# Between two decoder layers: block sums on VectorE, a fifth leading pair, ascending pool groups and two more buffers

## The chip, the cores and the metric

The kernel runs on one core of a Trainium2 chip. The metric is the device time of one execution in microseconds, the median of several. TensorE (PE) multiplies; VectorE (DVE), ScalarE (ACT) and GpSimd (POOL) do the elementwise work; almost all transfers are issued from SyncE's queue (SP).

## The reference

Two decoder layers on x of 1024 positions by 1024 features, all in float32. Layer 0 mixes by differential attention, layer 1 by causal pooling; both add attention over 256 memory tokens, gate the result and project it back onto the residual h.

```python
def multiscale_pool(u, w_group, scale):      # 4 groups of 384 columns, windows 2, 4, 8, 16
    ...
    outs.append((c - lag) / cnt - ug)        # mean over the window, less the value itself
    mixed = jnp.einsum('bsgc,gcd->bsgd', pooled, w_group)
    return mixed.reshape(B, S, MIX_WIDTH) * scale

for i in range(DEPTH):
    hn = rms_norm(h, ln_g[i])
    proj = jnp.einsum('bsd,de->bse', hn, w_in)        # splits into u, q_mem and gate
    y = diff_attention(u, ...) if i == 0 else multiscale_pool(u, ...)
    m = memory_attention(q_mem, mem_n, mem_w_kv[i])
    z = jnp.concatenate([y, m], axis=-1) * jax.nn.silu(gate)
    h = h + jnp.einsum('bse,ed->bsd', z, w_out[i])
return rms_norm(h, final_g)
```

## The kernel before

**Numbers.** Each float32 operand is split into a rounded part (a cast on ScalarE) and the rest (a subtraction on VectorE or GpSimd). A product is three matmuls, high by high, low by high, high by low: `mm3`, lines 125 to 127. Operands are held with features on partitions, and the 1024 positions in two halves of 512, called 0 and 1.

**Order.** The program of TensorE is written out by hand: `run_jobs` plays a list of jobs step by step, and loads what the next job needs before the present one runs. `play` puts units of memory attention in between at given step numbers (`starts`), counted from the start of the stage. The instructions of the other engines and of the DMA queues are put in order by a scheduler that simulates times; `high_priority(offset=SOON)` moves some ahead. Each engine and each queue then works in order.

**Stages.** Attention over 12 heads; memory attention of layer 0 (`memory_layer`); the output projection of layer 0 (`out_jobs(0)`); then layer 1 (`plan_mixing`): its input projection, memory attention, pooling and groups; the output projection of layer 1.

**Output projection.** For half 1 and then half 0, three rounds: output tiles 0 and 1 (two PSUM banks, `oa`), 2 to 5 (four banks, `ob`), 6 and 7 (`oc`). A round walks over 16 tiles z in chunks of 24 matmuls. A two-bank chunk uses one 512 KB weight tile and four z tiles, a four-bank chunk one weight tile and two z tiles. A z tile is loaded from DRAM into a `zf` buffer (256 KB, `nf` buffers) and split into a `zr` buffer (`nz`). `finish` adds the residual to an output tile, squares it (L514) and adds the squares up (L518).

**Layer 1's input projection.** It multiplies 2x2 blocks with seven products instead of eight (Winograd's form of Strassen's scheme), two weight tiles at a time: a *pair* has the products n = 1 ("11"), 2 ("21"), 6 ("t2"), 7 ("t3"), 5 ("t1"), 4 ("t4"), 3 ("22"). The names in brackets are blocks of the normed hidden state, or their sums. "11" and "21" come from half 1 alone (`blocks_first`). The others need half 0 too: `blocks_second` scales half 0's eight tiles (L1243), forms sums (L1266, L1267, L1269, L1270) and splits 20 blocks (L1235, L1236). A product is 12 matmuls in four steps; its weight operand is a *box*, prepared four products ahead (`prep`, L1106 and L1107).

Half 0's norm is known only when the first output projection has ended. To give TensorE work meanwhile, products 1 and 2 of four *first* pairs (memory queries and their gates) lead the stage; between them `row_means` (L250) and `row_spread` (L530) turn half 0's sum of squares into a factor `bc`. In order of jobs: p0: 1, 2; means; p1: 1, 2; spread; p2: 1, 2; p3: 1, 2; then 6, 7, 5, 4, 3 of each. Then the groups 3, 2, 1, 0 (windows 16, 8, 4, 2): pair (u, u), pair (gate, u), group part 0, pair (gate, gate), parts 1 and 2. `pooled_keep` pools a tile u as soon as both halves are there, with sums of doubling reach (L1381), and splits it (`ph`, L1395; `pl`, L1396). A group multiplies it and stores z (L1431, L608).

The second output projection reads the z tiles 12 to 15 in its first chunk, then 0 to 3, 4 to 7, 8 to 11.

## Time and profile before

| | us |
|---|---|
| median of 3 runs (1902.23 to 1903.84) | 1902.81 |
| profiled execution | 1894.44 |
| its span | 1892.7 |
| TensorE busy | 1760.5 |
| VectorE busy | 1338.9 |
| ScalarE busy | 951.6 |
| GpSimd busy | 746.0 |

The granted clock of TensorE was 0.973 on average. In the rows below, a line of a timeline gives start, duration, engine, source line, operation, output and inputs, shape and count, and in brackets the idle time of the engine before it with what ended it. A line of the waits gives who waited for whom, microseconds in all, times and the longest. A line of the stretches gives start and end, length, and per engine the busy time with the number of instructions, then clock, DMA share and GB/s.

### The profile page before, as it was taken

To read this page: it belongs to the slowest core of one execution; us is meant where nothing else is said; L and a number is where in the kernel's file an instruction comes from. 1 tells how busy PE (TensorE), PEld (TensorE's weight loads), DVE (VectorE), ACT (ScalarE), POOL (GpSimd) and SP (SyncE) were. 2 spreads that over 40 slices of the span, in tenths; PEclk is the share of its full clock that TensorE was granted. 3 is DMA by queue.
4 is the path that set the end of the run, shared out by engine and by line. 5 is a ranking of instruction groups with operands and counts; after the bars stand their busy time and mean duration, and the time that the engine had idled before them with its cause. 6 is when DMAs were issued, how large, how long until landed. Compare 5 with 4: busy or idle time off the path is not lost. (4 is left out here: it accounts for less than half of the span.)

```text
span 1892.7 us, 24833 instructions
## 1 busy us (share of the span) xinstructions
PE 1760.5 (93%) x8478; PEld 1452.4 (77%) x8478; DVE 1338.9 (71%) x2608; ACT 951.6 (50%) x1765; POOL 746.0 (39%) x660
## 2 busy tenths in 40 slices
PE   6999999999999999999899988968998999989997
PEld 5788888888888888887787766746776787768886
DVE  7778889888978888876566567677766767644413
ACT  6667657756765765643355445444432233324422
POOL 5334434444444434433344333463332424322452
PEclk9999999999999999999999999988998999999998
DMA  5101111111111111123626776622221121246542
GB/s 180 34 25 55 45 50 52 36 54 46 56 45 45 46 45 51 51 71 125 195 97 216 233 255 204 219 100 84 78 70 49 65 86 65 75 132 223 178 145 95
DMA packets 81536, 188.16 MB, mean 99 GB/s; under 512 B 9184, under 2 KB 17088, under 8 KB 81408
## 3 DMA queue, kind: packets, MB, share of 16 engines
q1 hardware_dynamic: 80016, 184.13, 29.6%
q10 hardware_dynamic: 1296, 2.17, 0.3%
q8 instruction: 67, 1.10, 0.2%
q14 instruction: 61, 0.50, 0.1%
q0 software_dynamic: 96, 0.26, 0.0%
HBM read 154.76 MB, written 31.77 MB: 99 GB/s over the span
## 5 line engine op out<-in xcount | busy, mean ns | idle before, releaser
L860 ACT ACTIVATE e<-e,st 128x640 f32<-128x640 f32 (+4 forms) x192 | 148.1, 773 | 112.3 <-DVE st L851 111.4
L118 POOL TENSOR_TENSOR wl_o<-wf_o,wh_o 128x384 fp32r<-128x384 f32 x64 | 97.0, 1516 | 226.0 <-ACT wh_o L115 196.3
L872 POOL TENSOR_SCALAR e<-e,st 128x640 f32<-128x640 f32 (+4 forms) x96 | 76.3, 795 | 199.8 <-DVE st L871 116.1
L1512 DVE TENSOR_TENSOR zr<-zf,zr 128x512 fp32r<-128x512 f32 x132 | 109.8, 851 | 60.5 <-ACT zr L1511 59.8
L118 DVE TENSOR_TENSOR wl_o<-wf_o,wh_o 128x640 fp32r<-128x640 f32 x64 | 61.0, 954 | 103.7 <-ACT wh_o L115 92.2
L1511 ACT CAST zr<-zf 128x512 fp32r<-128x512 f32 x132 | 80.9, 618 | 101.0 <-DMA zf<-z 83.2
L115 ACT CAST wh_o<-wf_o 128x1024 fp32r<-128x1024 f32 x64 | 67.2, 1049 | 120.0 <-PE ob L126 54.4
L900 ACT CAST wth<-wt 128x512 fp32r<-128x512 f32 (+2 forms) x168 | 72.4, 431 | 103.9 <-PE wt L897 74.1
L851 DVE CUSTOM_DVE_ANT_0 e<-s,mask 128x512 f32<-128x512 f32 (+2 forms) x192 | 109.6, 582 | 10.5 <-PE s L846 9.0
L125 PE MATMUL ga<-hh,wh_ga 128*128 128x512 f32 x256 | 104.1, 407 | 3.5 <-DVE mqf L620 3.5
L127 PE MATMUL ga<-hh,wl_ga 128*128 128x512 f32 x256 | 101.2, 395 | 0.0
L126 PE MATMUL ga<-hl,wh_ga 128*128 128x512 f32 x256 | 100.9, 394 | 0.0
L126 PE MATMUL ob<-zr,wh_o 128*128 128x512 f32 x256 | 100.1, 391 | 0.0
L125 PE MATMUL ob<-zr,wh_o 128*128 128x512 f32 x256 | 100.0, 391 | 0.0
L127 PE MATMUL ob<-zr,wl_o 128*128 128x512 f32 x256 | 99.6, 389 | 0.0
L846 PE MATMUL s<-kb,qa 128*128 128x512 f32 (+2 forms) x288 | 98.3, 349 | 1.1 <-DVE kb L798 1.1
L846 PE MATMUL s<-kb,qlo 128*128 128x512 f32 (+2 forms) x288 | 98.1, 348 | 0.0
L125 PE MATMUL k<-hh,wh_k 128*128 128x512 f32 x192 | 79.2, 413 | 9.0 <-ACT wh_k L115 9.0
L901 DVE TENSOR_TENSOR wtl<-wt,wth 128x512 fp32r<-128x512 f32 (+2 forms) x168 | 82.9, 493 | 6.1 <-ACT wth L900 4.7
L875 DVE SCALAR_TENSOR_TENSOR e<-e,st,e 128x640 f32<-128x640 f32 (+4 forms) x96 | 77.9, 811 | 9.9 <-POOL e L872 9.2
L897 PE MATMUL wt<-cst,e 128*128 128x128 f32 x432 | 69.9, 276 | 15.0 <-DVE e L875 12.6
L125 PE MATMUL v<-hh,wh_v 128*128 128x512 f32 x192 | 79.5, 414 | 0.0
(1227 smaller groups left out, 5749.2 us busy)
## 6 DMA issues: line engine op xcount, KB each, us to landing
zf<-z SPq DMA_DIRECT2D x132, 256.0 KB, 4.0
wf_o<-in_w_out SPq DMA_DIRECT2D x64, 512.0 KB, 3.5
wf_ga<-in_w_in SPq DMA_DIRECT2D x16, 512.0 KB
wf_q<-in_w_in SPq DMA_DIRECT2D x12, 512.0 KB, 3.2
wf_v<-in_w_in SPq DMA_DIRECT2D x12, 512.0 KB, 4.1
z<-rs SPq DMA_DIRECT2D x24, 256.0 KB, 3.3
z<-z SPq DMA_DIRECT2D x24, 256.0 KB, 2.0
z<-pz SPq DMA_DIRECT2D x24, 256.0 KB, 2.0
```

What stands on the lines that cost most here:

```text
L118: eng.tensor_tensor(wl[:, c], wf[:, c], wh[:, c].bitcast(F32), op=ALU.subtract)
L125: nc.tensor.matmul(out, sh, mh, start=first, stop=False, skip_group_check=more)
L126: nc.tensor.matmul(out, sh, ml, start=False, stop=False, skip_group_check=more)
L127: nc.tensor.matmul(out, sl, mh, start=False, stop=last, skip_group_check=more)
L846: nc.tensor.matmul(sc[m][:, w], q[half][part][:, m, qs], k[kh][:, m, w], start=(part == 0), stop=(part == 1),)
L851: nc.vector.tensor_tensor_reduce(out=es[m][:, lo:hi], in0=sc[m][:, : hi - lo], in1=self.mask[:, S - n + lo : S - n + hi], scale=1.0, scala ...
L860: nc.scalar.activation(es[m][:, :n], es[m][:, :n], AF.Exp, bias=least[m], scale=-1.0, accum_out=st[:, 2, m : m + 1],)
L872: nc.gpsimd.tensor_scalar(es[1][:, :n], es[1][:, :n], st[:, 3, 1:2], 1.0, op0=ALU.mult, op1=ALU.mult)
L875: nc.vector.scalar_tensor_tensor(es[0][:, :n], es[0][:, :n], st[:, 3, 0:1], es[1][:, :n], op0=ALU.mult, op1=ALU.add)
L901: nc.vector.tensor_tensor(wl[:, lo:hi], t[:, lo:hi], wh[:, lo:hi].bitcast(F32), op=ALU.subtract)
L1511: nc.scalar.copy(z[:, 0, :], zf)
L1512: nc.vector.tensor_tensor(z[:, 1, :], zf, z[:, 0, :].bitcast(F32), op=ALU.subtract)
```

## The change

- `mem_scores`: the scaling of the weights goes from GpSimd to VectorE (both layers).
- `plan_mixing`: a fifth leading pair, `lead` = (u0, u1). Its products 1 and 2 follow those of the four first pairs; its other five stand where the first group's first pair was. The means come after p0's first product, the spread after p1's first. The boxes of the leading products, and all boxes of the first two pairs, are split on VectorE. The groups go 0, 1, 2, 3.
- `keep`: the copies and sums kept between products get high priority; the lead pair keeps its first product in the pool of u.
- `blocks_second`: everything on VectorE, in the order in which the products use the blocks, with high priority; it reads the factor from PSUM instead of a copy.
- `pooled_keep`: until the buffers of the mixing stage are open, a pooling is put off (`late`).
- The starts of the memory units are moved in both layers.
- `out_jobs`: for layer 0, four zf and six zr buffers instead of three and five, two buffers for squares instead of one, and the last three squares of half 0 are added on VectorE.

```diff
         for i in range(4):
-            nc.gpsimd.tensor_scalar(
+            nc.vector.tensor_scalar(
                 e[:, i, :], e[:, i, :], st[:, 2, i : i + 1], 0.5, op0=ALU.mult, op1=ALU.mult
...
-        firsts = [self.pair(mq1(m), gate1(NH + m)) for m in range(MH)]
+        firsts = [self.pair(mq1(m), gate1(NH + m), m < 2) for m in range(MH)]
+        lead = self.pair(u1(0), u1(1))
+        lead["home"] = lambda: (self.upool, "p1", 1)
+        for p in firsts + [lead]:
+            p["early"] = (1, 2)
         for i, p in enumerate(firsts):
             self.product(p, 1)
-            self.product(p, 2)
             if i == 0:
                 self.between(lambda: means0(0))
             if i == 1:
                 self.between(lambda: spread0(0))
+            self.product(p, 2)
         self.mark("out0")
+        self.product(lead, 1)
+        self.product(lead, 2)
         for p in firsts:
             for n in (6, 7, 5, 4, 3):
                 self.product(p, n)
...
-        for gi in (3, 2, 1, 0):
+        for gi in range(4):
             t = 3 * gi
-            pairs(u1(t), u1(t + 1))
-            if gi == 3:
+            if gi == 0:
+                for n in (6, 7, 5, 4, 3):
+                    self.product(lead, n)
                 self.mark("mem1")
+            else:
+                pairs(u1(t), u1(t + 1))
             pairs(gate1(t), u1(t + 2))
...
-            self.split_box(box, f, HALF, nc.vector if n in (6, 3, 5) else nc.gpsimd)
+            by = nc.vector if n in (6, 3, 5) or p["vector"] or early else nc.gpsimd
+            self.split_box(box, f, HALF, by)
...
         def keep(name, a, b=None):
-            t = self.epool.tile([P, HALF], F32, tag="ev", bufs=6, name=f"{name}{nm}")
...
+            pool, tag, bufs = p["home"]() if name == "p1" and "home" in p else (self.epool, "ev", 6)
+            t = pool.tile([P, HALF], F32, tag=tag, bufs=bufs, name=f"{name}{nm}")
+            with self.tc.high_priority(offset=SOON):
+                self.land(t, a, b)
             p[name] = t
...
     def blocks_second(self, bc):
...
+        by = nc.vector
+        t2 = []
         for d, f in self.scale_hidden(0, bc):
             if d < 4:
                 continue
             i = d - 4
-            x11, x21, x12, x22 = h[1, i], h[1, d], h[0, i], h[0, d]
-            t2 = self.opool.tile([P, HALF], F32, tag="tt", bufs=2, name=f"t2_{i}")
-            nc.vector.tensor_tensor(x11, x12, x11, op=ALU.subtract)
-            nc.vector.tensor_tensor(t2, x22, x11, op=ALU.subtract)
-            self.split_block("t2", i, t2, 16 + 2 * i, 17 + 2 * i, (nc.gpsimd, nc.vector)[i % 2])
-            nc.gpsimd.tensor_tensor(x21, x21, t2, op=ALU.subtract)
-            nc.gpsimd.tensor_tensor(x12, x22, x12, op=ALU.subtract)
+            x11, x12, x22 = h[1, i], h[0, i], h[0, d]
+            t2.append(self.opool.tile([P, HALF], F32, tag="zf", bufs=4, name=f"t2_{i}"))
+            by.tensor_tensor(x11, x12, x11, op=ALU.subtract)
+            by.tensor_tensor(t2[i], x22, x11, op=ALU.subtract)
+            self.split_block("t2", i, t2[i], 16 + 2 * i, 17 + 2 * i, by)
         for i in range(4):
-            self.split_block("t3", i, h[0, i], 24 + 2 * i, 25 + 2 * i, nc.vector)
+            by.tensor_tensor(h[0, i], h[0, 4 + i], h[0, i], op=ALU.subtract)
+            self.split_block("t3", i, h[0, i], 24 + 2 * i, 25 + 2 * i, by)
         for i in range(4):
-            self.split_block("t1", i, h[1, i], 48 + 2 * i, 49 + 2 * i, nc.vector)
+            self.split_block("t1", i, h[1, i], 48 + 2 * i, 49 + 2 * i, by)
         for i in range(4):
-            self.split_block(
-                "t4", i, h[1, 4 + i], 44 + i, 40 + i, (nc.gpsimd, nc.vector)[i % 2]
-            )
+            by.tensor_tensor(h[1, 4 + i], h[1, 4 + i], t2[i], op=ALU.subtract)
+            self.split_block("t4", i, h[1, 4 + i], 44 + i, 40 + i, by)
         for i in range(4):
-            self.split_block("22", i, h[0, 4 + i], 32 + i, 36 + i, nc.vector)
+            self.split_block("22", i, h[0, 4 + i], 32 + i, 36 + i, by)
...
                 return
+            if self.late is None:
+                pooled(u)
+            else:
+                self.late.append(lambda: pooled(u))
...
-                self.mpool, 0, self.gates[0][NH:], [94, 101, 108, 114, 120, 126, 132, 138]
+                self.mpool, 0, self.gates[0][NH:], [100, 105, 111, 116, 122, 127, 133, 138]
...
-                            self.mpool, 1, self.gates[1][NH:], [14, 38, 31, 57, 54, 78, 74, 95],
+                            self.mpool, 1, self.gates[1][NH:], [22, 47, 39, 70, 63, 92, 85, 106],
...
                     with self.pool("mix") as self.xpool:
+                        for fn in self.late:
+                            fn()
+                        self.late = None
                         self.drain("mix")
...
-        nf, nz = ((3, 5), (4, 20))[layer]
+        nf, nz = ((4, 6), (4, 20))[layer]
...
-            last = layer == 1 and half == 0 and d > 4
+            last = half == 0 and d > 4
             self.accumulate_square(
-                pool, h, ssum[half], d, nm, (("ssum", 1), ("ssum_", 1), ("sqt", 1 if layer == 0 else 2)),
+                pool, h, ssum[half], d, nm, (("ssum", 1), ("ssum_", 1), ("sqt", 2)),
                 alone=layer == 1 and half == 0,
                 add=nc.vector if last else None,
             )
...
+            if layer == 0 and half:
+                bc = self.opool.tile([P, HALF], F32, tag="bc", name=f"bc{half}")
+                self.blocks_first(self.keep_spread(half, bc))
+                return
             if layer == 0:
-                bc = self.opool.tile([P, HALF], F32, tag="bc", name=f"bc{half}")
-                (self.blocks_second, self.blocks_first)[half](self.keep_spread(half, bc))
+                with self.tc.high_priority(offset=SOON):
+                    self.blocks_second(self.row_spread(half))
                 return
```

More of the change, by code (lines that the diff above doesn't have):

```diff
@@ L1075, in plan_mixing, with pair @@
             self.group(gi, 2)
-    def pair(self, first, second):
-        return {"specs": (first, second)}
+    def pair(self, first, second, vector=False):
+        return {"specs": (first, second), "early": (), "vector": vector}
     def entry(self, prep, run, fetch=lambda: None):
@@ L1124, in product @@
         k0, k1 = slice(0, HALF), slice(HALF, D)
-        early = n in (1, 2) and name0.startswith("pmq")
+        early = n in p["early"]
         def fetch():
@@ L1166, in keep @@
         def keep(name, a, b=None):
-            t = self.epool.tile([P, HALF], F32, tag="ev", bufs=6, name=f"{name}{nm}")
-            if b is None:
-                nc.scalar.copy(t, a)
-            else:
-                nc.vector.tensor_tensor(t, a, b, op=ALU.add)
+            pool, tag, bufs = p["home"]() if name == "p1" and "home" in p else (self.epool, "ev", 6)
+            t = pool.tile([P, HALF], F32, tag=tag, bufs=bufs, name=f"{name}{nm}")
+            with self.tc.high_priority(offset=SOON):
+                self.land(t, a, b)
             p[name] = t
@@ L1374, in evac, with pooled @@
                 return
+            if self.late is None:
+                pooled(u)
+            else:
+                self.late.append(lambda: pooled(u))
+        def pooled(u):
             pool = self.xpool
@@ L1460, in other_layers @@
         self.hid = {}
+        self.late = []
         with self.pool("blocks") as self.h2pool, self.pool("boxes") as self.spool:
```

## The prediction

> **What bounds the kernel now.** I read the page first, for the busy shares and the slices, then the waits of TensorE from 990 us on, then a table of stretches cut at the borders of the stages, and last the timeline around each long wait.
>
> ```profile
> PE 1760.5 (93%) x8478; PEld 1452.4 (77%) x8478; DVE 1338.9 (71%) x2608; ACT 951.6 (50%) x1765; POOL 746.0 (39%) x660
> PEclk9999999999999999999999999988998999999998
> 1230.00 0.39 PE L125 MATMUL pmq_pga12x<-x11h,box 128*128 128x512 f32 x1
> 1232.49 0.39 PE L127 MATMUL pmq_pga12x<-x11h,box 128*128 128x512 f32 x1
> ```
>
> TensorE is the bound, and the clock row is below 9 in slices 27 and 28 (1230 to 1325 us, the seam between the layers), 31 and the last. The two matmuls are the first and the twelfth of one product: eleven starts in 2.49 us, so an undisturbed 512-column matmul costs 0.227 us, a product of twelve 2.72 us, and a chunk of the output projection (24 matmuls) 5.45 us. Against that pace the stretches are measured.
>
> ```profile
> core 0: us, PE busy (x) PEld busy (x) DVE busy (x) ACT busy (x) POOL busy (x), PEclk, DMA share, GB/s
> 1229.80:1297.40 67.60, 45.86 (x162) 33.36 (x160) 50.52 (x68) 28.11 (x56) 37.90 (x25) 0.75 0.26 86
> 1020.10:1047.40 27.30, 23.89 (x97) 18.65 (x97) 17.43 (x21) 12.53 (x19) 9.15 (x6) 0.95 0.73 237
> 1047.40:1092.00 44.60, 44.60 (x196) 36.60 (x195) 27.23 (x31) 21.39 (x31) 15.70 (x10) 0.99 0.67 222
> 1092.00:1120.60 28.60, 23.60 (x96) 17.33 (x95) 15.95 (x20) 13.02 (x20) 10.65 (x8) 1.00 0.78 261
> 1120.60:1159.40 38.80, 27.36 (x113) 20.17 (x112) 30.08 (x43) 20.19 (x32) 15.10 (x10) 0.93 0.59 199
> 1204.00:1229.80 25.80, 23.16 (x96) 17.24 (x95) 15.13 (x18) 12.82 (x20) 11.96 (x9) 1.00 0.71 243
> 1297.40:1407.30 109.90, 100.82 (x484) 80.61 (x485) 75.49 (x119) 46.42 (x114) 36.96 (x45) 0.98 0.26 83
> 1407.30:1689.40 282.10, 264.95 (x1141) 214.74 (x1141) 193.00 (x242) 87.84 (x140) 99.87 (x76) 0.98 0.21 69
> ```
>
> The first row is the seam: eleven products (30.0 us), the two small row-sum steps (2 us) and one set of scores (1.4 us), 33.4 us of work in 67.6: 34 us lost. The next five are the first output projection. Its middle rounds (1047 to 1092, eight chunks, 43.6 us) lose 1 us; the rounds of two banks (four chunks, 21.8 us) lose 5.5, 6.8, 17.0 and 4.0. The last row holds 1140 matmuls, 259 us, and loses 23.
>
> ```profile
> PE oa L126 <- DVE zr L1512: 12.1, 8, 6.5
> PE oa L125 <- ACT zr L1511: 10.8, 5, 8.1
> PE grp L125 <- ACT ph L1395: 6.9, 1, 6.9
> PE pmq_pga15x L125 <- ACT p1pmq_pga L1169: 6.6, 1, 6.6
> PE pmq_pga12y L126 <- POOL xt2l L1236: 6.3, 2, 4.3
> PE mt L681 <- POOL me L672: 4.5, 5, 1.5
> ```
>
> Six causes, each of which the diff touches.
>
> **Part 1, the seam.** What PE waits for is the block sums, and these run slowly because VectorE and GpSimd work side by side.
>
> ```profile
> 1234.53 0.64 ACT L514 ACTIVATE ssq<-hn 128x512 f32<-128x512 f32 x1 [1.03 <-POOL ssq L518]
> 1241.19 0.50 PE L125 MATMUL pmq_pga13x<-x21h,box 128*128 128x512 f32 x1 [0.67 <-ACT p1pmq_pga L1169]
> 1245.24 0.59 ACT L538 COPY bc<-bc_h 128x512 f32<-128x512 f32 x1
> 1245.87 6.03 DVE L1243 SCALAR_TENSOR_TENSOR hn<-hn,gains,bc 128x512 f32<-128x512 f32 x8 [2.06 <-ACT bc L538]
> 1260.83 3.43 POOL L1270 TENSOR_TENSOR hn<-hn,hn 128x512 f32<-128x512 f32 x2
> 1263.03 1.77 DVE L1236 TENSOR_TENSOR xt1l<-hn,xt1h 128x512 fp32r<-128x512 f32 x1
> 1282.84 0.68 DVE L1236 TENSOR_TENSOR xt4l<-hn,xt4h 128x512 fp32r<-128x512 f32 x1
> 1283.44 0.68 DVE L1236 TENSOR_TENSOR x22l<-hn,x22h 128x512 fp32r<-128x512 f32 x1
> ```
>
> A subtraction takes 1.77 us while GpSimd runs two in 3.43 us, and 0.68 us, started every 0.60, when GpSimd rests. The sums take from 1245.9 to 1285 us. The change puts all 44 instructions (8 scalings, 16 sums, 20 splits) on VectorE: 44 x 0.60 = 26.6 us. It also puts there the squares of the last three tiles (3 x 0.68), so the row sum no longer waits 1.03 us for GpSimd; it asks for the means one product earlier and for the spread one product earlier (2.7 us), and reads the spread from PSUM, without the copy. Three products (8.2 us) and the two small steps (2 us) from 1230.0: the scalings start at about 1240.3 instead of 1245.9.
>
> The copy dropped is 0.59 us.
>
> ```profile
> L1219 DVE SCALAR_TENSOR_TENSOR gap<-tanhp,gap x24: 678/693/2401, 1301.1 to 1682.9; 128x512 f32<-128x512 f32 x24
> L1219 DVE SCALAR_TENSOR_TENSOR gap<-tanhp,pga_u11x x1: 675/675/675, 1416.9 to 1416.9; 128x512 f32<-128x512 f32 x1
> ```
>
> With an operand in PSUM the same form takes 0.675 us, with both in SBUF 0.693, so eight scalings from PSUM cost nothing more and I book -0.6 us. The Trainium skill, page "VectorE: DVE Perf Modes", section "Rules for kernel authors", advises to copy a matmul output to SBUF first when many operations read it, and its cycle table adds 62 cycles to a PSUM source, an estimated 0.06 us each; by that the sum would be -0.1 instead of -0.6. No row here shows the surcharge.
>
> Until the sums are there, PE has the rest of the first products: after the spread, 7 products instead of 4 (p1's second, two each of p2, p3 and of the new fifth pair), 19 us, to 1261. The fifth pair's two products are moved, not added: 5.45 us. With them go one more 512 KB load on SP (its weights are read again later), two casts and two copies on ACT, two splits on VectorE; the load lies beside DMA that is 0.26 busy, and costs nothing; if it came late, some 4 us, by the landings in part 2. "t2", the first block needed, is 20 instructions: 12 us, plus some 4 us of box splits: 1257, in time. From then on VectorE is behind. To the last product of the first pair (ideal start 1272) it owes 26.6 + 12 box preparations (7.2) + three evacuations and a set of memory scores (about 4.5) = 38.3 us from 1240.3: 1278.6. So I leave 6.6 us of waiting, 2 us of bank waits (0.67, the row at 1241.19, for each of the three pairs whose two products still follow each other), 0.5 for the squares, 3 for ScalarE's queue: 12 in place of 34. Minus 0.6 already in that, the term is **-22**, bounds 0 (nothing starts earlier) and -34.
>
> **Part 2, the first output projection.** zf buffers 3 to 4, zr 5 to 6.
>
> ```profile
> zf<-z SPq DMA_DIRECT2D x88, 256.0 KB, 3.8
> 1148.13 8.42 DVE L1243 SCALAR_TENSOR_TENSOR hn<-hn,gains,bc 128x512 f32<-128x512 f32 x8
> 1157.21 0.79 PE L126 MATMUL oa<-zr,wh_o 128*128 128x512 f32 x1 [6.53 <-DVE zr L1512]
> ```
>
> A zf buffer is busy for its landing (3.8 us) and the cast and subtraction (0.62 + 0.69, with little queueing): 5.3 us. A two-bank chunk eats four in 5.45 us; three buffers give four in 7.1, a loss of 1.6 us a chunk, 6.5 a round, near the 5.5 and 6.8 seen. Four buffers give four in 5.3. The transport must then carry 1.5 MB per 5.45 us, 275 GB/s, where these rounds show 237 to 261 at a DMA share of 0.73 to 0.78, so landings get slower: of 16.3 us in three rounds I take 9, of the fourth's 17 (2 of them small steps) 4. The 6.5 us there come from eight scalings of the other half ahead of a zr on VectorE, which the diff leaves: 0. Term **-13**, bounds 0 and -29.
>
> **Part 3, memory attention.** In the first layer the units start six steps later; a step of the key projection is six matmuls of 256 columns.
>
> ```profile
> 945.77 0.58 PE L125 MATMUL ms<-mkvr,mq 128*128 128x256 f32 x1 [4.46 <-ACT mkvr L645]
> 952.48 2.41 POOL L672 TENSOR_SCALAR me<-me,mst 128x256 f32<-128x256 f32 x4 [9.87 <-DVE mst L670]
> 939.92 0.42 DVE L425 TENSOR_TENSOR mkf<-mk,rsmb 128x256 f32<-128x256 f32 x1 [0.36 <-PE mk L127]
> ```
>
> At half of 0.227 us each a step is 0.68 us, six are 4.1: the 4.46 us wait is filled with work that stands there anyway: **-4**, bounds 0 and -4.5. The scaling of the weights goes to VectorE, 64 instructions, each at most 0.42 us (the two-operand row of that size) and at least 0.15; I take 0.3, so 1.2 us for a unit instead of 2.4. The 4.5 us of transposes waiting for GpSimd in the second layer mostly go; VectorE is 0.69 busy there (75.5 of 109.9) and gains 10 us of these and 4 of splits, which gives some back: **-2**, bounds +4 and -4.5.
>
> **Part 4, ascending groups.** The pooling of window 16 moves from the first group to the last, with its gate and z stores.
>
> ```profile
> 1405.60 2.41 POOL L1381 TENSOR_TENSOR ws<-u 128x1039 f32<-128x1039 f32 x1 [2.23 <-DVE u L1197]
> 1435.22 0.79 PE L125 MATMUL grp<-ph,box 128*128 128x512 f32 x1 [6.87 <-ACT ph L1395]
> 1692.84 4.70 SPq L608 DMA_DIRECT2D z<-pz  x4
> 1698.41 1.82 SPq L1510 DMA_DIRECT2D zf<-z  x4
> 1703.22 0.80 PE L125 MATMUL oa<-zr,wh_o 128*128 128x512 f32 x1 [8.06 <-ACT zr L1511]
> ```
>
> Two poolings one after the other fill VectorE from 1405.6 to 1435, longer than the 19 us pair beside them; that comes back in the last group, so the 6.87 us wait moves: 0, bounds +3 and -7. The first group has window 2, deferred until its pool of buffers opens, 24 steps (16 us) ahead of its use: hidden; without that cover some 6 us for each of its two poolings (the 2.41 us sum and four steps more). At the end the second projection's second chunk reads tiles 0 to 3, three of which are stored last, on SP right ahead of their loads. Ascending, 9 to 11 are last, needed two chunks (10.9 us) later, so the loads pass the stores: 8.06 us and 2 of slow clock, of which I leave 3: **-7**, bounds 0 and -10.
>
> **Sum.** -22 - 13 - 4 - 2 - 7 = -48 against the profiled execution of 1894.4 us (span 1892.7), which lies 8.4 below the median of 1902.8; on the median: **1855 us**.
>
> **Rivals.** (a) VectorE's lateness in the seam comes as one long wait, and the clock falls. For: the 6.53 us wait above is followed by a 0.79 us matmul, and the clock is 0.75 over the seam. Then the first pair's five products (60 matmuls) run at the slow pace, about 0.43 us for 0.227: +12, and 6 more of waiting: 1873. Against: the wait expected comes in pieces of 1 to 3 us. The Trainium skill, page "TensorE: Matmul & The Clock Gate", Part 1, has half rate after an idle window of about 3.4 us and full rate after a busy one of that length; by that rule this case hangs on whether one piece is that long, and the 6.53 us row agrees. (b) The edit does not do what it says to the projections: transport or order on SP, not buffers, sets them. For: the DMA share of 0.78. Against: slices without such waits at equal demand in the second projection. Parts 2 and 4 then give nothing: 1875. (c) Slower: GpSimd's remaining work lies beside VectorE's. From 1229.8 to 1689.4 VectorE is busy 319 us; it gains about 30, loses 16 of lengthened subtractions: 333, against at most 393 of matmuls (33, 101 busy, 259) and 460 elapsed. The forecast ends slower than now once its instructions there take 1.45 times as long (484 us: 460 and the 24 gained elsewhere). For: 1.77 against 0.68. Against: GpSimd, 175 us busy there, loses work. Price at 1.5 (500 us): 1919.
>
> **Numbers.** Forecast 0.63 (1840 to 1870 in itself), (a) 0.17, (b) 0.14, (a) with (b) 0.02 (1893), (c) 0.04. Range 1834 to 1884: it takes in (a) and (b) and the better ends of parts 1 and 2 in part. About 0.2% (4 us) is what a measurement of this kernel can tell from no change: faster 0.94, same 0.02, slower 0.04.
>
> **What would show it.** Part 1: no GpSimd instruction among the block sums, subtractions at 0.68, TensorE's clock over 0.9 in the seam. Part 2: two-bank rounds of 24 us. Part 3: no wait of the first scores. Part 4: no wait for zr at the second projection's second chunk, and one for ph at the last group. Wrong it is if box splits stand behind the sums on VectorE and PE waits in the first products, or if SP still issues the zf loads behind the last stores.

## The result, and the profile after

The changed kernel takes 1850.36 us (median of 4 runs, 1847.53 to 1853.36) against 1902.62 us before: a ratio of 0.9724, interval 0.9704 to 0.9745. 1855 was predicted. The profiled execution took 1847.82 us, with a span of 1846.0 us, 46.7 less than before's 1892.7.

First the page of the changed kernel: busy time by engine, and TensorE's granted clock in 40 slices.

```profile
PE 1744.3 (94%) x8478; PEld 1449.0 (78%) x8478; DVE 1353.1 (73%) x2701; ACT 948.6 (51%) x1764; POOL 660.7 (36%) x567
PEclk9999999999999999999999999999999999989998
```

The 8s of slices 27 and 28, the seam, are gone, and so is that of slice 31 (the wait for ph before). The 8 in slice 36 (1615 to 1661 us) is new and holds the wait of the second output projection, which stood at 1695 to 1703 us before; the last slice is as it was. Next the table of stretches of the changed kernel: the seam, the six rounds of the first output projection, the rest of the first pairs with the memory attention, the mixing, and the second output projection. The columns are those of the table in the prediction.

```profile
1206.20:1271.20 65.00, 50.36 (x223) 39.61 (x222) 56.97 (x106) 32.86 (x65) 0.15 (x2) 0.92 0.32 106
1019.60:1041.35 21.75, 21.75 (x97) 17.99 (x96) 15.54 (x21) 11.96 (x20) 6.61 (x4) 1.00 0.79 263
1041.35:1084.90 43.55, 43.55 (x194) 36.06 (x193) 28.28 (x33) 20.89 (x31) 14.05 (x10) 1.00 0.73 241
1084.90:1107.40 22.50, 22.03 (x97) 17.91 (x96) 17.18 (x20) 13.43 (x21) 11.56 (x8) 1.00 0.95 321
1107.40:1132.85 25.45, 24.43 (x114) 19.58 (x112) 19.57 (x36) 16.01 (x25) 8.88 (x6) 1.00 0.91 307
1132.85:1184.40 51.55, 45.71 (x193) 37.07 (x192) 39.44 (x42) 24.21 (x36) 21.53 (x14) 0.93 0.60 197
1184.40:1206.20 21.80, 21.80 (x97) 18.02 (x97) 16.45 (x21) 12.09 (x19) 8.49 (x6) 1.00 0.79 271
1271.20:1358.10 86.90, 83.54 (x417) 68.56 (x416) 70.28 (x135) 40.10 (x104) 12.26 (x9) 0.98 0.29 97
1358.10:1640.90 282.80, 267.54 (x1147) 216.26 (x1146) 194.29 (x245) 87.43 (x141) 103.68 (x76) 0.99 0.21 69
1640.90:1846.00 205.10, 184.41 (x809) 151.50 (x807) 75.45 (x116) 69.28 (x95) 71.84 (x50) 0.94 0.51 166
```

The same borders in before are in TensorE's program: the first matmul of the memory keys, of the first output projection, of the first pair, of the second pair's product 6 (where the seam ends here), of the first group's second pair, of the second output projection. Before, the stretch of the seam read so; the old seam in the prediction ended at 1297.4, a product earlier.

```profile
1230.00:1306.40 76.40, 54.04 (x200) 39.79 (x199) 57.73 (x78) 31.87 (x62) 41.89 (x28) 0.78 0.25 83
1306.40:1407.30 100.90, 92.44 (x447) 74.01 (x446) 68.08 (x108) 42.66 (x108) 32.98 (x40) 0.98 0.27 86
```

| stage (us) | before | after | difference | work moved taken out | predicted |
|---|---|---|---|---|---|
| start to the memory keys | 913.5 | 914.4 | +0.9 | | 0 |
| memory keys to first output projection (part 3, layer 0) | 106.7 | 105.2 | -1.5 | | -4 |
| first output projection (part 2) | 209.8 | 186.6 | -23.2 | | -13 |
| seam (part 1) | 76.4 | 65.0 | -11.4 | -16.8 | -22 |
| rest of the first pairs (part 3, layer 1) | 101.0 | 86.9 | -14.1 | -7.2 | -2 |
| mixing and second output projection (part 4) | 485.3 | 487.9 | +2.6 | +1.2 | -7 |
| sum | 1892.7 | 1846.0 | -46.7 | | -48 |

"Work moved" is, first, the lead pair's two products, 5.45 us, which the change carries from the stage behind the seam into it. Second, it is six matmuls of the last memory units (`mo`), 1.4 us, which ran before the border of the mixing and now run behind it: 1141 matmuls stand in the mixing's row before, 1147 here. The sum is right within 2 us and no term is right within 2 us: the errors cancel, and that is luck. The waits of TensorE in the changed kernel from 900 us on show what is left.

```profile
PE u_u1x L125 <- ACT p1u_u L1204: 11.7, 1, 11.7
PE oa L125 <- ACT zr L1531: 8.3, 1, 8.3
PE ob L126 <- DVE zr L1532: 5.3, 1, 5.3
PE grp L125 <- ACT ph L1411: 4.4, 1, 4.4
```

The first line is new: one wait of 11.7 us in the seam. The second is the wait of the second output projection, unmoved (8.1 before). The third is the 6.5 us wait behind the eight scalings, which is now in the next round. Beside those two long ones, the two `oa` lines for zr of before held 5.6 us (VectorE's) and 2.7 us (ScalarE's) of shorter waits, in the two-bank rounds. These are gone, and so are the 6.3 for xt2l; of the 6.6 for p1, 0.7 is left.

### The profile page after: what moved, and what is told of

It reads as the page before. It is cut to its first block, busy times and chain, and to the rows that moved or that the text cites. A ratio compares the mean times of both kernels' runs of the same rounds, so it can differ in the third digit from the quotient of the medians.

```text
span 1846.0 us, 24825 instructions
## 1 busy us (share of the span) xinstructions
PE 1744.3 (94%) x8478; PEld 1449.0 (78%) x8478; DVE 1353.1 (73%) x2701; ACT 948.6 (51%) x1764; POOL 660.7 (36%) x567
## 4 chain that ended last, share of the span: by engine, by line
PE 69%; DVE 17%; ACT 5%; DMA 5%; issue 3%; POOL 1%; SPq 0%; DVEq 0%; ACTq 0%; POOLq 0%
PE s L846 4%; PE o L920 3%; PE ob L127 3%; PE ob L126 3%; PE ob L125 3%; PE ga L125 3%; PE ga L127 3%; PE ga L126 3%; PE v L127 2%; PE v L125 2%; PE v L126 2%; PE wt L897 2%; PE q L125 2%; PE q L127 2%; PE q L126 2%
## 5 line engine op out<-in xcount | busy, mean ns | idle before, releaser
L115 ACT CAST wh_o<-wf_o 128x1024 fp32r<-128x1024 f32 x64 | 67.2, 1050 | 108.6 <-PE ob L126 61.2
L897 PE MATMUL wt<-cst,e 128*128 128x128 f32 x432 | 69.4, 274 | 13.9 <-DVE e L875 11.5
```

The source lines that it names most:

```text
L897: nc.tensor.transpose(t[:, c : c + P], w[b][:, j * P : (j + 1) * P], self.ident)
```

## The experiments

The ratios below are to the kernel before, measured beside each run, with their 95% intervals; the changed kernel's is 0.9724. The start of the memory keys lay between 911.9 and 918.7 us in the profiled executions of all the kernels below, though the code up to there is the same in all of them. So stages are compared, and the time from the memory keys to the end: 979.2 us before, 931.6 in the changed kernel. Stages with the same code differ too from one profiled execution to the next: the first layer's memory stage took 103.8 to 106.3 us, the first output projection 186.6 to 190.9, the seam 64.9 to 66.3, the rest of the first pairs 84.6 to 87.8, the mixing 282.4 to 283.8, the second projection 203.9 to 207.5. What lies inside these spreads is not read as an effect.

**Buffers of the first output projection.**

```diff
-        nf, nz = ((4, 6), (4, 20))[layer]
+        nf, nz = ((3, 5), (4, 20))[layer]
```

(The t2 tiles, which need four buffers, get two in zf's place and two elsewhere.)

> The changed kernel with three zf and five zr buffers again in the first output projection; all else stays. Theory (a zf buffer is busy 5.3 us, so three give four tiles in 7.1 us where a chunk has 5.45): the two-bank rounds, now 21.8, 22.5, 25.4 and 21.8 us, go back to about 27, 28, 32 and 26; seam start 1206 becomes about 1225, the time 18 to 23 us longer. Rival (the squares added on VectorE and the second buffer for squares made the rounds shorter): rounds stay within 2 us, the time at most 5 us longer.

1870.83 us (ratio 0.9837, interval 0.9818 to 0.9856). The stretches of its four two-bank rounds:

```profile
1015.85:1040.75 24.90, 23.13 (x97) 17.76 (x96) 15.95 (x22) 12.31 (x19) 6.62 (x4) 1.00 0.73 242
1084.85:1112.45 27.60, 24.07 (x98) 17.59 (x97) 17.85 (x21) 13.13 (x20) 11.82 (x8) 1.00 0.80 268
1112.45:1152.05 39.60, 28.60 (x114) 21.36 (x113) 30.05 (x43) 20.28 (x33) 16.24 (x10) 0.90 0.59 199
1196.85:1222.43 25.58, 23.43 (x98) 17.80 (x97) 15.56 (x22) 12.89 (x20) 9.00 (x6) 1.00 0.74 254
```

The projection takes 206.6 us instead of 186.6. Against the spread of this stage, 16 to 20 of the 23.2 us belong to the two extra buffers. Whether the rest belongs to what the diff changes besides (two buffers for squares, three squares on VectorE) or to the spread was not split further. Rival (b), transport or order, falls for this projection: with four buffers two rounds moved 321 and 307 GB/s where 237 to 261 had been seen.

**Order of the groups.**

```diff
-        lead = self.pair(u1(0), u1(1))
+        lead = self.pair(u1(9), u1(10))
...
-        for gi in range(4):
+        for gi in (3, 2, 1, 0):
...
-            if gi == 0:
+            if gi == 3:
```

> The changed kernel with the groups in descending order 3, 2, 1, 0 and the lead pair (u9, u10) instead of (u0, u1). Theory (ascending order gained nothing, as the wait of the second projection stayed 8.3 us): the time within 3 us of the changed kernel, the zr wait 8 us in both. Rival (ascending order is worth what window 16 costs in the first group, whose pooling must wait until the buffers of the mixing stage open): 4 to 9 us longer, with a wait for ph of 5 to 8 us in the first group.

1855.70 us (0.975, 0.9732 to 0.9768); from the memory keys to the end it takes 937.5 us, 5.9 more than in the changed kernel. Of these, 4.2 lie in the mixing, and the rest in stages whose code is the same. In the waits of this kernel:

```profile
PE oa L125 <- ACT zr L1531: 8.6, 1, 8.6
PE grp L125 <- ACT ph L1411: 6.9, 1, 6.9
PE pga_u11v L125 <- DVE u L1206: 2.9, 1, 2.9
```

The wait for ph is 6.9 us instead of 4.4, and one of 2.9 us stands by window 16's pooling in the first group: the mixing takes 287.0 instead of 282.8. The wait of the second projection is the same in both orders, 8.6 and 8.3. So the gain of the order lies where I had booked 0, and there is none where I had booked -7.

**Scaling of the memory weights.**

```diff
-            nc.vector.tensor_scalar(
+            nc.gpsimd.tensor_scalar(
                 e[:, i, :], e[:, i, :], st[:, 2, i : i + 1], 0.5, op0=ALU.mult, op1=ALU.mult
```

> The changed kernel with the scaling of the memory weights on GpSimd again, in both layers. Theory (the 8.6 us gained between the second pair and the first mixing pair came from this scaling): 5 to 9 us longer, waits of the transposes for GpSimd back at about 4 us. Rival (they came from the new starts of the units): within 2 us, few such waits. In the first layer's memory stage the waits for mkvr on VectorE (1.5 and 1.1 us) would get shorter, 1 to 2 us gained.

1853.01 us (0.9736, 0.9719 to 0.9753). In the second layer the wait comes back, and the seam and the stage behind it are 2.2 us longer each (67.2 and 89.1):

```profile
PE mt L681 <- POOL me L672: 3.6, 5, 1.1
```

In the first layer it is the other way: from the memory keys to the projection it takes 102.1 us, with VectorE 105.2, and the waits there for mkvr's split on VectorE are 0.8 instead of 3.0 us. So GpSimd is the better place in the first layer. On VectorE four of these scalings take 1.14 us in the changed kernel's seam, 0.28 each where 0.3 was estimated.

**Starts of the first layer's memory units.**

```diff
-                self.mpool, 0, self.gates[0][NH:], [100, 105, 111, 116, 122, 127, 133, 138]
+                self.mpool, 0, self.gates[0][NH:], [94, 101, 108, 114, 120, 126, 132, 138]
```

> The changed kernel with the first layer's memory units at their old starts (94, 101, ...). Theory (later starts removed the 4.5 us wait, but closer starts made two new ones of 1.5 and 1.1 us): the 4.5 us wait is back and those two are gone, the time within 2 us. Rival (the new waits come from the scaling on VectorE): both the 4.5 us wait and the new ones, 3 to 5 us longer.

1857.31 us (0.9758, 0.9739 to 0.9778). The memory stage takes 108.5 us, 3.4 more than in the changed kernel and 1.9 more than before. The wait is back, longer than the 4.46 of before, and the shorter waits for mkvr's split are gone:

```profile
PE ms L125 <- ACT mkvr L645: 6.6, 2, 5.9
```

So the later starts gave about 3 of the 4 us of my step, and the scaling on VectorE took most of it away again, as the 3 us of the run before it also show. The median says 7 us longer, which neither side had expected; the stage accounts for 3.4 of it, and 3.7 lie in the first output projection, within its spread.

**Block sums on both engines again** (4 sums of t3, 4 of t4 and half of the splits of t2 and t4 on GpSimd).

```diff
-            by.tensor_tensor(h[0, i], h[0, 4 + i], h[0, i], op=ALU.subtract)
+            nc.gpsimd.tensor_tensor(h[0, i], h[0, 4 + i], h[0, i], op=ALU.subtract)
...
```

> The changed kernel with the sums of t3 and t4 (8) and half of the splits of t2 and t4 (4) on GpSimd again; order and priority stay. Theory (VectorE and GpSimd side by side lengthen each other's instructions): subtractions of 1.2 to 1.8 us on VectorE again, seam (first product to the second pair's sixth) from 65 to 72 us or more, 6 to 15 us longer. Rival (VectorE's work is the bound of the seam, and 12 instructions or 7 us less on it help): 2 to 7 us shorter.

1861.23 us (0.9788, 0.9764 to 0.9812); the seam takes 72.6 us instead of 65.0. From its timelines, GpSimd and VectorE:

```profile
1225.64 12.25 POOL L1282 TENSOR_TENSOR hn<-hn,hn 128x512 f32<-128x512 f32 x4 [24.25 <-DVE hn L1278]
1237.85 1.73 POOL L1287 TENSOR_TENSOR hn<-hn,t 128x512 f32<-128x512 f32 x1
```

```profile
1230.30 1.28 DVE L1279 TENSOR_TENSOR t<-hn,hn 128x512 f32<-128x512 f32 x2
1233.99 1.10 DVE L1245 TENSOR_TENSOR xt3l<-hn,xt3h 128x512 fp32r<-128x512 f32 x1 [1.80 <-ACT xt3h L1244]
1235.01 1.75 DVE L1245 TENSOR_TENSOR xt1l<-hn,xt1h 128x512 fp32r<-128x512 f32 x1
1257.89 0.68 DVE L1245 TENSOR_TENSOR x22l<-hn,x22h 128x512 fp32r<-128x512 f32 x1
```

These are as many sums and splits as GpSimd had before the change. Twelve instructions were moved off VectorE, and yet its last split starts 50 us behind the start of this kernel's seam (1207.9) instead of 44: while GpSimd runs at 1.73 us each, VectorE's subtractions take 1.75 instead of 0.68. It does not begin at once. GpSimd's first sum is on record from 1225.64 on, and VectorE keeps its 0.60 apiece beside it; only when VectorE has paused 1.80 us for a cast do both run at 1.7.

**Four leading pairs instead of five** (the lead pair's products 1 and 2 back at their old place).

```diff
-        self.product(lead, 1)
-        self.product(lead, 2)
...
-                for n in (6, 7, 5, 4, 3):
+                for n in (1, 2, 6, 7, 5, 4, 3):
                     self.product(lead, n)
```

> The changed kernel with four leading pairs: the fifth pair's first two products stand back with its other five; all else stays, so the memory units of layer 1 start at the same step numbers. Theory (the fifth pair's products run into a queue on ScalarE, so their 5.45 us cover nothing): within 2 us of the changed kernel. Rival (they cover 5.45 us of the wait for the sums): 4 to 6 us longer.

1855.78 us (0.9754, 0.9734 to 0.9775). Seam and the stage behind it take 157.5 us together, 151.9 in the changed kernel: the pair saves 5.6 us, about its own 5.45 us of work. Without it the wait is for t2 itself:

```profile
PE pmq_pga12y L126 <- DVE xt2l L1243: 5.8, 4, 3.4
```

**Copies of the first products on VectorE.** The 11.7 us wait is for a copy on ScalarE of a product whose last matmul starts at 1235.28. ScalarE's timeline in the changed kernel shows why it comes so late:

```profile
1238.34 0.62 ACT L1244 CAST xt4h<-hn 128x512 fp32r<-128x512 f32 x1 [0.18 <-DVE hn L1287]
1241.95 1.22 ACT L1244 CAST xt4h<-hn 128x512 fp32r<-128x512 f32 x2 [2.99 <-DVE hn L1287]
1246.22 0.62 ACT L1115 CAST box<-s2pmq_pga 128x512 fp32r<-128x512 f32 x1 [3.05 <-DVE s2pmq_pga L1153]
1246.75 0.58 ACT L1204 COPY p1u_u<-u_u1x 128x512 f32<-128x512 f32 x1
```

ScalarE stands idle twice for 3 us, with the copy queued behind casts that wait for VectorE's sums.

```diff
-                self.land(t, a, b)
+                if b is None:
+                    nc.vector.tensor_copy(t, a)
+                else:
+                    self.land(t, a, b)
```

> The changed kernel with the copy of each pair's first product on VectorE instead of ScalarE. Theory (the one long wait of the seam, 11.7 us, is a 0.58 us copy standing behind casts in ScalarE's queue): the wait goes to 0 to 2 us, the next wait is for the blocks of t2 (last split 1243.7) and box of product 6, about 3 to 5 us; 5 to 8 us gained. Rival (VectorE's total work of the block sums is the bound, the copy only shows it first): the wait moves to product 6 or 7 in full, at most 3 us gained.

1856.65 us (0.9758, 0.9734 to 0.9781), seam 67.2, and the mixing, where the copies of the other pairs are moved too, 286.7. My theory fell: the wait moves to earlier pairs and is no shorter, 13.8 us together. Nor did the rival's wait at product 6 or 7 come.

```profile
PE pmq_pga15x L125 <- DVE p1pmq_pga L1181: 9.5, 1, 9.5
PE pmq_pga14x L125 <- DVE p1pmq_pga L1181: 4.3, 1, 4.3
```

**The last group's stores on another queue.**

```diff
-                        self.store_z(1, t, half, z)
+                        self.store_z(1, t, half, z, nc.scalar if gi == 3 else nc.sync)
...
```

> The changed kernel with the z stores of the last group issued from ScalarE's queue instead of SP. Theory (the loads of tiles 0 to 3 for the second chunk of the second projection wait only because they stand behind the last group's stores on SP): the loads are issued before 1643, the 8.3 us wait for zr goes to 0 to 2 us, 6 to 10 us gained. Rival (the loads wait for memory or for the weight buffer that is loaded ahead of them): they stay near 1650 and the wait stays at 7 to 9 us.

1848.08 us (0.9721, 0.9699 to 0.9744), from the memory keys to the end 931.6 as in the changed kernel. The wait for zr is 8.7 us and SP's queue shows the loads where they were:

```profile
1642.74 7.34 SPq L104 DMA_DIRECT2D wf_o<-in_w_out  x2
1650.18 2.07 SPq L1530 DMA_DIRECT2D zf<-z  x4
```

The stores in front of the loads do not hold them. In both kernels a weight load stands right ahead, the fifth of this projection where a round has four, so one of the next round. In the changed kernel's queue:

```profile
1645.47 3.83 SPq L608 DMA_DIRECT2D z<-pz  x4
1649.75 0.33 SPq L104 DMA_DIRECT2D wf_o<-in_w_out  x1
1650.20 1.99 SPq L1530 DMA_DIRECT2D zf<-z  x4
```

**Loads of the second projection ahead.** In the program these loads belong to a pool of buffers that opens when the mixing's pools close. This run issues them earlier, into slots of the block tiles, which the last pair frees.

```diff
-                return w, [operand(half, r, korder[kk * nk + k2]) for k2 in range(nk)]
+                zs = [operand(half, r, korder[kk * nk + k2]) for k2 in range(nk)]
+                if layer == 1 and half == 1 and widx == 0:
+                    for t in korder[4:12]:
+                        operand(half, r, t)
+                return w, zs
...
-            if layer == 1 and half == 1 and r == 0 and t in korder[:4]:
+            if layer == 1 and half == 1 and r == 0 and t in korder[4:12]:
+                i = korder.index(t) - 4
+                zf = self.slot(i, f"zf{nm}", F32)
+                z = Parts(self.slot(16 + 2 * i, f"zh{nm}"), self.slot(17 + 2 * i, f"zl{nm}"))
...
```

> The 16 operand loads of the second projection's second and third chunks (tiles 0 to 7 of the half computed first) are issued with those of its first chunk, before the last group is done, into slots of the block tiles, which the last pair frees by 1624 us; nothing else changes. Theory (the 8.3 us wait for zr stays in the changed kernel because these loads stand on SP behind a weight load of a later chunk and behind the memory of the closing pools, not behind the stores of the last group's z; ascending order is the condition for issuing them early, since tiles 0 to 7 are stored three groups or one group before): the 8.3 us wait goes, the fourth chunk's tiles 8 to 11 (still loaded at about 1650) are needed 16 us later, so the time is 5 to 9 us below the changed kernel's. Rival (the transport or ScalarE's and VectorE's casts at the end of the last group set the time, not the order): the wait turns into one of similar length for the casts or for the weights, and the time stays within 2 us.

1837.71 us (0.9683, 0.9655 to 0.9711). TensorE has no wait left between 1630 and 1700; the stretch of the first 58.1 us of the projection, here and then in the changed kernel:

```profile
1641.90:1700.00 58.10, 58.10 (x257) 47.99 (x256) 26.33 (x37) 24.41 (x34) 18.11 (x12) 1.00 0.76 256
```

```profile
1640.90:1699.00 58.10, 49.76 (x207) 40.10 (x206) 25.35 (x35) 22.38 (x32) 14.78 (x10) 0.91 0.70 238
```

50 matmuls more in the same time; the projection takes 193.5 us instead of 205.1, 11.6 less where 5 to 9 were expected. The loads are issued from 1615 on instead of 1650. That was the cause: the place of the loads in the program and the buffers that go with it, not the stores. Which of the two held them, the weight load ahead on SP or the pool that opens late, this run does not separate, since it changes both. Ascending groups suit it, since tiles 0 to 7 are then stored before the last group; descending groups with another order of reading were not tried.

**Casts behind VectorE's sums taken off ScalarE.**

```diff
-        self.nc.scalar.copy(h, f)
+        if name == "t4":
+            self.nc.vector.tensor_copy(h, f)
+        else:
+            self.nc.scalar.copy(h, f)
...
```

(And the cast of the box of product 3 in VectorE's two pairs.)

> The four casts of the block t4 and the cast of the third product's box in VectorE's own two pairs go from ScalarE to VectorE, right behind the sums that they wait for. Theory (the seam's 11.7 us wait is ScalarE's queue: the copy of the lead pair's first product, whose matmuls end at about 1235.5, stands behind casts that wait 3 us each for VectorE's late sums): with no such cast ahead of it the copy runs at about 1238, the second product of the lead pair by 1239, and the next wait is for t2, whose last split is at 1243 plus what the moved casts add to VectorE (5 of 0.4 to 0.7 us, 2 to 3.5 us): the 11.7 us become 1 to 3 for the copy and 3 to 5 for t2, the seam 4 to 7 us shorter, 1844 to 1847 us. Rival (VectorE's own lateness sets the seam, and ScalarE's queue only shows it): the sums end later by the added casts, the wait moves to t2, t3 and t4, and the seam is the same or up to 4 us longer.

1852.93 us (0.9765, 0.9732 to 0.9797); the seam takes 69.6 us, 4.6 more. The copy comes at 1238.2, as the theory said, and the next wait eats it; the waits, then ScalarE's timeline:

```profile
PE pmq_pga12z L125 <- ACT u L1204: 13.9, 1, 13.9
PE u_u1x L125 <- ACT p1u_u L1204: 2.5, 1, 2.5
```

```profile
1238.17 0.58 ACT L1204 COPY p1u_u<-u_u1x 128x512 f32<-128x512 f32 x1
1251.63 0.62 ACT L645 CAST mkvr<-mkv 128x512 fp32r<-128x512 f32 x1 [12.88 <-DMA mkv<-mv]
1258.90 0.62 ACT L645 CAST mkvr<-mkv 128x512 fp32r<-128x512 f32 x1 [6.10 <-DMA mkv<-mv]
1259.42 0.58 ACT L1204 COPY u<-u_u1x 128x512 f32<-128x512 f32 x1
```

The copy of the lead pair's second product (`u`) stands on ScalarE behind the casts of the memory keys, and these wait for loads that stand on SP behind weight loads, issued at 1245.4 and 1246.9. SP's waits from 1234 to 1249 name VectorE's splits of boxes (10.3 us) and its sums for them (1.2): the buffers of these weights come free when VectorE is through with them, near the end of its sums.

**All three together.** Loads ahead, casts on VectorE, and the scaling of the memory weights on GpSimd in the first layer and on VectorE in the second.

```diff
-            nc.vector.tensor_scalar(
+            (nc.gpsimd, nc.vector)[int(nm[0])].tensor_scalar(
...
```

> Both edits of the two runs before it, and the scaling of the memory weights on GpSimd in the first layer and on VectorE in the second. Theory (the three places are separate stages and add up): the first layer's memory attention is 2 to 4 us shorter than in the changed kernel (102 instead of 105 us from the first memory key to the first output projection), the seam and the second projection are as in the two runs alone, and the time is 8 to 18 us below the changed kernel's. Rival (what is taken from one stage comes back in the next, VectorE's queue being the common limit): less than 4 us below.

1835.90 us (0.9675, 0.964 to 0.971). The first layer's memory stage takes 100.6 us instead of 105.2, the second projection 193.5, the seam 66.5: the gains of the stages add up, and from the memory keys to the end it is 916.4 us, 15.2 less than the changed kernel. The seam, where the casts are, has no part in that gain. The wait for u is 8.0 us here instead of 13.9, and the seam 3.1 us shorter than in the run of the casts alone; why was not followed up.

**Memory loads on GpSimd's queue**, on top of that.

```diff
-        nc.sync.dma_start(f[:, 0:MEM], self.mk_dram[layer][h])
+        by = nc.gpsimd if layer else nc.sync
+        by.dma_start(f[:, 0:MEM], self.mk_dram[layer][h])
...
```

> The combined kernel (loads of the second projection ahead, five casts on VectorE, memory weights on GpSimd in the first layer and on VectorE in the second), and in the second layer the memory keys, values and queries are loaded from GpSimd's queue instead of SP's. In the combined kernel the lead pair's first copy came in time, and a wait of 8.0 us (13.9 in the run of the casts alone) took its place: the copy of its second product stands on ScalarE behind the cast of the memory keys, which waits 13 us for a load that SP issues behind two weight loads; these wait for buffers that VectorE frees at the end of its sums. Theory (that chain, ScalarE behind SP behind VectorE, is what still holds the seam): the load is issued some 15 us earlier, the 8.0 us wait goes, the next is for VectorE's splits at 2 to 4 us, and the seam is 4 to 8 us shorter than the combined kernel's 66.5: 1828 to 1832 us. Rival (VectorE's late sums themselves set the seam, and each wait in front of them only shows it): the wait moves on to t2, t3 or t4 at the same length, the seam stays within 2 us of 66.5, and GpSimd's queue, in which the box splits of the later pairs now stand behind loads that wait for buffers, may cost up to 5 us behind the seam.

1833.47 us (0.9646, 0.9621 to 0.9671), the fastest median measured, though its interval overlaps the one of the run before it and from the memory keys to the end it is 917.0 us. The seam takes 67.2 us, as the rival had it, though its reason is not shown: no wait for t2, t3 or t4 took the place. The wait for u is 5.7 us here, and 2.8 us of waits for the memory keys' split on VectorE are new. The load is issued 37.6 us behind the start of the seam, in the combined kernel 40.5, so it came 3 us earlier and not 15, and the theory was hardly put to the test. In GpSimd's timeline the load leaves SP's queue only to stand behind a memset whose buffer VectorE frees with a split of t2:

```profile
1238.69 0.11 POOL L1383 MEMSET u<- 128x16 f32 x1 [43.71 <-DVE xt2l L1249]
1238.93 0.60 POOL L639 DMA_DIRECT2D mkv<-mk  x1
```

## Why the prediction was right in the sum and wrong in its terms

**Part 1, -16.8 for -22.** Half of the step held. GpSimd has 0.15 us in the seam (so rival (c), in which it slows VectorE down, fell), the sums run at 0.60 apiece, and the scalings start 11.1 us after the seam does (10.3 were predicted). (44 x 0.60 is 26.4 us and not 26.6, which changes nothing.) The rows are the scalings, the last split of t2 and the last splits of all:

```profile
1217.30 5.36 DVE L1252 SCALAR_TENSOR_TENSOR hn<-hn,gains,bc_h 128x512 f32<-128x512 f32 x8 [1.78 <-PE bc_h L530]
1243.05 0.68 DVE L1245 TENSOR_TENSOR xt2l<-t,xt2h 128x512 fp32r<-128x512 f32 x1
1249.67 1.28 DVE L1245 TENSOR_TENSOR x22l<-hn,x22h 128x512 fp32r<-128x512 f32 x2
```

The Trainium skill, page "VectorE: DVE Perf Modes", section "Rules for kernel authors", offers two ways for a matmul's output: to accept the slow mode, or to copy it to SBUF first if many operations follow. The eight scalings from PSUM take 0.743 us each, and those of before from SBUF 0.74 (without the first, which ran beside GpSimd), so here the dropped copy is a gain. The block sums on VectorE alone are worth some 7 us (7.6 in the run above), the fifth pair 5.6 us.

The step that failed is the 12 us left of the 34: "6.6 us of waiting", "2 us of bank waits", "0.5 for the squares, 3 for ScalarE's queue". Bank waits are 1.4 and squares 0.7, but ScalarE's queue is not 3: it is one wait of 11.7 us. I counted the work in each queue, and not what a queue does when its head waits for another engine. The sum's remainder was thus 17 instead of 12. A second step failed beside it and was hidden by this wait: t2 was to be there 16 us behind the first scaling ("20 instructions: 12 us, plus some 4 us of box splits: 1257, in time"). Its last split ends 26.4 us behind it. The program names the blocks in the order of their use, but on VectorE the scheduler put sums and splits of t1, t3 and t4 ahead of t2's last split. Without the wait for the copy, TensorE would have been through the lead pair at about 1239 and would have waited for t2 until about 1243.7, an estimate from these rows; the run with four leading pairs shows such waits, 5.8 us.

Four runs tried to remove this wait: copies on VectorE, casts on VectorE, and, in the combined kernels, loads off SP. Each time the wait named was gone or shorter and another took its place, and the seam took 66.5 to 69.6 us, never less than the changed kernel's 65.0. This speaks for VectorE's sums (to 1251), with everything that stands behind them in order, as what holds the seam; so does the run with the sums on both engines, where they end 6 us later and the seam is 7.6 longer. It is not shown: no run made the sums earlier, and how short the seam could be with a different order of all three queues was not tried.

Rival (a) said that one long wait would come and the clock would fall for five products, +12 us. The wait came; the price did not:

```profile
1247.38 0.79 PE L125 MATMUL u_u1x<-x21h,box 128*128 128x512 f32 x1 [11.71 <-ACT p1u_u L1204]
1250.53 0.43 PE L126 MATMUL u_u1x<-x21l,box 128*128 128x512 f32 x1
```

Seven starts in 3.15 us, then 0.23 again: 1.6 us lost to the clock. The Trainium skill, page "TensorE: Matmul & The Clock Gate", Part 1, has full rate after a busy window of about 3.4 us. The 3.15 us are near that; after the 8.3 us wait of the second projection the slow pace lasted longer, from 1654.97 to 1660.40. My price took the old seam's 0.75 for the state after one wait, while it came of waits that kept returning: in before's seam TensorE waited 6.6, 4.3, 2.2, 2.0 and 2.9 us between 1254 and 1283.

**Part 2, -23.2 for -13.** The mechanism was right, 7.1 us for four tiles with three buffers and 5.3 with four: two-bank rounds take 21.75, 22.5, 25.45 and 21.8 us. The term that was mis-sized is what the transport would take back, 7 of 16 us: I took the 237 to 261 GB/s seen as near a limit (and the 275 needed are 289, with the 262,144 bytes of a 256 KB tile). Counted from the first matmul of a round to that of the next, the three plain rounds gave 16.6 (27.6, 29.0 and 26.2 to 21.8, 22.6 and 21.8) where 9 were booked. The round with the scalings gave 13.5, and the next took back 7.3, which leaves 6 where 4 were booked: the 6.5 us wait behind eight scalings stayed, as said, but one round later and at 5.3.

**Part 3.** Layer 0: -1.5 for -4. The wait of the first scores went, but four scalings on VectorE ahead of the splits cost 3 us: a term missing from the first layer, where I had costed the move for the second only. Layer 1: -7.2 for -2. With the scaling back on GpSimd this stage is 2.2 us longer, and the seam another 2.2, which belongs to part 1's stage. What gave the other 5 was not isolated; fewer splits on a GpSimd that runs beside VectorE is a guess.

**Part 4, +1.2 for -7.** The step that failed: "9 to 11 are last, needed two chunks (10.9 us) later, so the loads pass the stores". I ordered the loads by their data. They were tied to a pool that opens after the mixing, and stood on SP behind a weight load of the next round, so the order of the stores changed nothing, and the wait is 8.3 us instead of 8.1. The prediction named this sign itself, and rival (b), order on SP, came true here. The other half, the wait for ph "moves: 0", was pessimistic: 6.9 became 4.4, at the last group. Without the six matmuls moved into it, the mixing is 0.7 us shorter than before. In the changed kernel ascending beats descending by 4.2 and yet gains only 0.7 against before, since with descending groups the mixing, counted the same way, is 3.5 longer than before's: 1.4 of it is the wait for u (2.9 instead of 1.5), the rest was not isolated. The second projection is 1.9 us longer, 205.1, and runs with the same code there took 203.9 to 207.5.

## What to carry to other kernels

Count for each queue not only its work but its head: an instruction that waits for another engine stops all that is behind it, and removing the wait that the profile names shows the next one in the same chain. For a buffer count, compare the turnaround of a buffer with the pace of the consumer; do not discount the gain by the bandwidth seen while that wait held it down. Here, reordering the producers paid at the consumer only once its loads could be issued earlier: see in the queue what stands ahead of them, and which pool's opening they wait for.

## What the runs showed of the hardware

- Two-input float32 operations of 128x512 on VectorE and GpSimd lengthen each other: VectorE takes 0.68 us alone and 1.75 beside GpSimd, GpSimd 1.29 alone (the changed kernel's box splits at 1276 and 1424) and 1.73 beside VectorE (the run with block sums on both). Moving twelve instructions to GpSimd made VectorE finish 6 us later. As long as VectorE ran without a pause, GpSimd's first sum did not slow it down: before the change that sum is on record for 7.06 us, from 1252.58 on, and VectorE stayed at 0.60 apiece until it paused at 1258.5.
- The 16 DMA engines carried 321 GB/s at a share of 0.95 for 22 us, where 268 GB/s at 0.80 was the most in the same round with one buffer fewer.
- A cast of 128x512 takes 0.41 us on VectorE (the run of the casts, at 1243.08; the next operation starts 0.33 later) and 0.62 on ScalarE.
- After a wait TensorE's matmuls of 512 columns started mostly every 0.43 us instead of 0.23, for 3.15 us after a wait of 11.7 us and for 5.4 after one of 8.3.
